# A blocked Strassen matmul with bias and tanh: three hand-set orders moved around the change from plain to Strassen work

## The chip, the cores and the metric

One core of a Trainium2 chip. The metric is the device time of one launch in microseconds (us), the median of three runs. An engine's "queue" is the order in which its instructions stand in the program: each engine takes them one after the other, and a waiting instruction holds up all behind it.

## The reference

```python
m, k, n = 4096, 4096, 4096
a: float32 [m, k];  b: float32 [k, n];  bias: float32 [n]
return np.tanh(np.matmul(a, b) + bias)
```

## The kernel before

The output is made in four column blocks of 1024 and sixteen row pairs of 256 rows. One such piece of 256 x 1024 is an **item** (`items`, indexed by `n`). An item is computed by Strassen's scheme in its Winograd-like form: seven products `m1` to `m7` of half size (128 x 2048 by 2048 x 512), each 16 matmuls on TensorE (PE), line 339. The left operands are the quarters `a11`, `a12`, `a21`, `a22` of the item's rows and their differences `s1`, `s2`, `s5`, `s6`, `s7` (`asum`, line 89, on VectorE, DVE); the right operands are `b11`, `b22` and the sums `d1`, `d3`, `d4`, `e6`, `e7`. `a11` and `a12` come from the first 128 rows of the item (`r = 0`), `a21` and `a22` from the second (`r = 1`).

Rows of `a` come from HBM by DMAs on GpSimd's queue (POOL), cast to float16 (`load_nat`, line 147): two tiles (`u` = 0, 1) of four DMAs each for every `r`. VectorE turns them (`turn`, `transpose`, line 174) into the layout that TensorE needs; each quarter takes a turn from `u` = 0 and one from `u` = 1. The tiles lie in the pool `wide` with eight buffers, which also holds the raw blocks `b12` and `b21`.

The first three row pairs of the first column block are computed plainly before any item, in the groups A, B and C of two row blocks each (`ROWS`), four row blocks at a time in the eight PSUM banks, while `b` still arrives. The visits follow `ORDER`; the last, to group A, is `last_visit`, in two parts (columns `j` = 0, 1) between the first item's products. When a row block is finished, `end(m, j)` applies tanh on ScalarE (ACT, line 671) into an output tile and stores it from SyncE's queue (SP, line 350). Output tiles come from `new_out()` (pool `outs`, three buffers) or from `narrow()`, which goes round the spare buffers of `temps` and `outs`.

What comes when is written by hand. Time is counted in **slots**: `at_slot(slot, f, ...)` lists work for a slot, and the main loop goes through the slots, emits the slot's listed work, then a visit if the slot is negative, and then the slot's products. Items stand 7 slots apart. Where several calls have the same slot, they come in the order in which they were listed. `prepare(n)` lists an item's loads, turns and sums:

```python
loads = {0: (-5, -4), 1: (0, 2), 2: (3, 5)}.get(n, (s0 - 7, s0 - 4))
for r in range(2):
    at_slot(loads[1 - r], load_nat, n, r)
```

The first two items (`n < LEAD`) have an order of products of their own: m4 (slot 7n), m2 (+2), m3 (+4), m1 (+5), m5 (+6), m6 (+8), m7 (+10). From the third item on it is m2 (7n), m5 (+2), m3 (+4), m1 (+5), m4 (+6), m6 (+8), m7 (+10). Products of neighbouring items interleave. After a product its banks are read out: `lead_after` and `lead_add` for the first two items, `after` for the others. For the third item, `after("m2")` puts two reads of m2's bank on VectorE (to `d` and to `s`), and m5 goes on accumulating in that bank only behind both. `lead_bias(n)` copies the bias into the bank of m4 on ScalarE; `lead_add(n)` adds m2's copy `zs` to it, applies tanh (`result`, line 359), stores it, and copies the bank to `ds`.

Of the kernel before, what the change touches and what calls it, by code (L numbers as in the profile page):

```python
# [8 lines left out]
P = 128  # L9
QP = 32  # L10
NB = 512
# [6 lines left out]
fp32 = mybir.dt.float32  # L18
# [5 lines left out]
TANH = mybir.ActivationFunctionType.Tanh  # L24
# [30 lines left out]
ROWS = {"A": (0, 1), "B": (2, 3), "C": (4, 5)}  # L55
# [5 lines left out]
def kernel(  # L61
# [7 lines left out]
    nc = tc.nc  # L69
# [11 lines left out]
    wide = ctx.enter_context(tc.tile_pool(name="wide", bufs=8))  # L81
# [39 lines left out]
    def again(n):  # L121
        return items[n][3]
# [38 lines left out]
    def quad(n, name):  # L161
        if name not in aset[n]:
            aset[n][name] = quads.tile([P, T, P], fp16, name=name, tag=name)
        return aset[n][name]

    def transpose(dst, src, lowest):

        nb = src.shape[2]
        split = [(0, nb, "P mb b (t x) -> P mb b t x")]
        if lowest:  # L170
            split = [(0, 1, "P mb b (x t) -> P mb b t x"), (1, nb - 1, split[0][2])]
        for b0, n, order in split:
            if n:
                nc.vector.transpose(  # L174
                    dst[:, ds(b0 * TB, n * TB), :].rearrange(
                        "P (b t) (mb p) -> P mb b t p", t=TB, p=QP
                    ),
                    src[:, :, ds(b0, n), :].rearrange(order, t=TB),
                )

    def turn(n, name, u):
        c, pairs, part, _ = items[n]
        r, h = int(name[1]) - 1, int(name[2]) - 1
        src = nat[n, r, u].rearrange("P mb (b h k) -> P mb b h k", h=2, k=TB * QP)[:, :, :, h, :]
        if part is None:
            dst = quad(n, name)[:, :, ds(u * 2 * QP, 2 * QP)]
        else:
            dst = quad(n, name)[:, ds(u * TP, TP), :]
        transpose(dst, src, h == 0 and not part)

    def stored(n, name):
        c, pairs, part, _ = items[n]
# [156 lines left out]
    def store(o, pair, r, c, j):  # L349
        nc.sync.dma_start(  # L350
            out=out[ds((2 * pair + r) * P, P), ds(c * NCW + j * NB, NB)], in_=o
        )

    def new_out():
        return outs.tile([P, NB], fp32, name="o", tag="o")
# [112 lines left out]
    def at_slot(slot, f, *args):  # L468
        work.setdefault(slot, []).append((f, args))

    def prepare(n):

        s0 = SLOTS * (n - 1)
        if again(n):
            at_slot(s0, lambda: aset[n].update((i, aset[n - 2][i]) for i in QUADS))
        elif natural(n):
            loads = {0: (-5, -4), 1: (0, 2), 2: (3, 5)}.get(n, (s0 - 7, s0 - 4))
            for r in range(2):
                at_slot(loads[1 - r], load_nat, n, r)
            turns = {  # L480
                0: (("a22", (-2, -1)), ("a21", (-2, -1)), ("a11", (2, 3)), ("a12", (2, 4))),
                1: (("a22", (5, 6)), ("a21", (5, 6)), ("a11", (8, 9)), ("a12", (8, 9))),
                2: (("a22", (10, 10)), ("a21", (11, 11)), ("a11", (12, 12)), ("a12", (13, 13))),
            }.get(n, [(i, (s0 + x, s0 + y)) for i, (x, y) in {
                "a22": (0, 0), "a21": (2, 2), "a11": (3, 4), "a12": (5, 5)
            }.items()])
            for name, at in turns:
                for u in range(2):
                    at_slot(at[u], turn, n, name, u)
                if n:  # L490
                    at_slot(at[1], keep, n, name)
        else:
            for name, at in (("a22", 0), ("a21", 1), ("a11", 2), ("a12", 4)):
                at_slot(s0 + at, fetch, n, name)
        late = stays(n)
        end_ = n == len(items) - 1
        sums_at = {"s2": 4, "s5": 6, "s1": 9}
        sums_at["s6"] = 12 if late else 13 if end_ else 8
        sums_at["s7"] = 15 if late else 12 if end_ else 13
        if n < LEAD:  # L500
            at_slot(s0 + 10, lead_add, n)
        if n == 0:
            sums_at = {"s2": 6, "s1": 10, "s5": 11, "s6": 14, "s7": 16}
        elif n == 1:
            sums_at = {"s2": 6, "s1": 9, "s5": 9, "s6": 13, "s7": 14}
        elif n == 2:
            sums_at.update({"s2": 5, "s5": 6})
        for name, at in sums_at.items():
            at_slot(s0 + at, asum, n, name)
# [20 lines left out]
    mb = {}  # L530
# [31 lines left out]
    def narrow(name):  # L562
        pool, tag = rest[taken[0] % len(rest)]
        taken[0] += 1
        return pool.tile([P, NB], fp32, name=name, tag=tag)
# [50 lines left out]
    for m in range(4):  # L616
        src = a[ds(m * P, P), :].rearrange("p (q k) -> p q k", q=4)[:, :, ds(0, TB * QP)]
# [4 lines left out]
        if m == 1:  # L622
            nc.gpsimd.affine_select(
                out=ident, in_=ident, compare_op=mybir.AluOpType.is_equal, fill=0.0,
# [4 lines left out]
    for t in range(0, TB, 2):  # L629
        for q in (0, 2, 1, 3):  # L630
            src = bass.AP(
                tensor=b.tensor, offset=b.offset + (q * KQ + t) * N,
                ap=[[TB * N, QP], [N, 2], [1, NCW]],
            )
# [31 lines left out]
            mb[m, j] = psum.tile([P, NB], fp32, name=f"ps_{2 * m + j}", tag=f"ps_{2 * m + j}")  # L666
    banks = [mb[i] for i in ((3, 0), (0, 0), (2, 1), (1, 0), (2, 0), (0, 1), (3, 1), (1, 1))]

    def end(m, j):
        o = new_out() if m in ROWS["A"] else narrow("o")  # L670
        nc.scalar.activation(o, mb[m % 4, j], TANH)
        store(o, m // 2, m % 2, 0, j)

    def visit(v):
        g = ORDER[v]
# [26 lines left out]
    def last_visit(j):  # L702
        for m in ROWS["A"]:
            down(m, j, 7 * TB, 8 * TB, stop=True)
            end(m, j)

    for slot, f, *args in (
        (-22, turn_in, "C0", (4, 5)),
        (-21, add_bias, 2, False), (-21, add_bias, 3, False),
        (-20, add_bias, 0, True), (-20, add_bias, 1, True),  # L710
        (-20, land, "C2", 4, TP, TP), (-20, opening_b, 3),
        (-19, turn_in, "B1", (2, 3), TB, TB), (-19, turn_in, "B1", (2, 3), TP, TB),
        (-18, turn_in, "A1", (0, 1), TB, TB), (-18, turn_in, "A1", (0, 1), TP, TB),
        (-17, land, "B3", 2, 3 * TB, TP), (-17, land, "A3", 0, 3 * TB, TP), (-17, opening_b, 4),
        (-17, add_bias, 4, True), (-17, add_bias, 5, True), (-17, bsum, "d4", 0),
        (-16, turn_in, "C2", (4, 5)),
        (-15, land, "C4", 4, T, TP), (-15, opening_b, 5),
        (-15, bsum, "d3", 0), (-15, bsum, "e6", 0), (-14, bsum, "d1", 0), (-14, bsum, "e7", 0),
        (-13, turn_in, "B3", (2, 3), 3 * TB, TB), (-13, turn_in, "B3", (2, 3), T, TB),
        (-13, turn_in, "A3", (0, 1), 3 * TB, TB), (-13, turn_in, "A3", (0, 1), T, TB),  # L720
        (-12, land, "B5", 2, 5 * TB, TP), (-12, land, "A5", 0, 5 * TB, TP), (-12, opening_b, 6),
        (-12, bsum, "d4", 1), (-12, bsum, "d3", 1), (-11, bsum, "e6", 1), (-11, bsum, "d1", 1),
        (-10, turn_in, "C4", (4, 5)), (-10, bsum, "e7", 1),
        (-9, land, "C6", 4, 6 * TB, TP), (-9, opening_b, 7),
        (-9, bsum, "d4", 2), (-8, bsum, "d3", 2), (-8, bsum, "e6", 2),
        (-7, turn_in, "B5", (2, 3)), (-7, turn_in, "A5", (0, 1)),
        (-6, land, "B7", 2, 7 * TB, TB),
        (-6, bsum, "d1", 2), (-6, bsum, "e7", 2),
        (-4, turn_in, "C6", (4, 5)), (-4, land, "A7", 0, 7 * TB, TB),
        (-3, bsum, "d4", 3), (-3, bsum, "d3", 3), (-3, bsum, "d1", 3),  # L730
        (-2, turn_in, "B7", (2, 3)),
        (0, turn_in, "A7", (0, 1)), (0, bsum, "e6", 3), (1, bsum, "e7", 3),
        (5, lead_bias, 1),
    ):
        at_slot(slot, f, *args)

# [3 lines left out]
    for c in range(1, NC):  # L740
        n = next(n for n in range(len(items)) if items[n][0] == c)
# [4 lines left out]
    for slot in range(1 - len(ORDER), SLOTS * len(items) + 4):  # L746
        for f, args in work.get(slot, ()):
            f(*args)
        if slot < 0:
            visit(slot + len(ORDER) - 1)  # L750
        elif slot in (1, 3):
            last_visit(slot // 2)
        for pos, p in PRODUCTS.items():
            n, r = divmod(slot - pos, SLOTS)
            if r == 0 and 0 <= n < len(items):
                if n < LEAD:
                    product(n, *PRODUCTS[FIRST[pos]])
                elif n < len(items) - 1 or p[0] not in ("m6", "m7"):
                    product(n, *p)
                elif p[0] == "m6":  # L760
                    product(n, *PRODUCTS[10])
                else:
                    last_product(n, *PRODUCTS[8][1:])
# [30 lines left out]
```

## Time and profile before

| | us |
|---|---|
| median of three runs (1578.27 to 1578.87) | 1578.69 |
| the profiled execution's own time | 1580.22 |
| its span | 1578.5 |
| TensorE busy in the span | 1569.0 |
| VectorE busy | 925.5 |
| GpSimd busy (issue of DMAs) | 354.8 |
| ScalarE busy | 286.6 |
| mean granted TensorE clock | 0.999 |

A row of a timeline gives start, length, engine, line, operation, written and read tile, and count; in brackets stands the idle time of the engine before it and what ended it. The name `ps` is any PSUM bank, `s` a difference of `a`, `a` a turned quarter, `nat` rows as they land.

### The profile page before, as it was taken

What the parts mean: (1) busy time and instruction counts of PE and PEld (TensorE: products, weight loads), DVE (VectorE), ACT (ScalarE), POOL (GpSimd) and SP (SyncE); (2) the same over time, 40 slices, a digit from 0 to 9 for tenths busy, and PEclk for the clock granted to TensorE, in tenths of its full rate; (3) what the DMA queues carried; (4) which work ended last, traced back from release to release, by engine and by line L of the source; (5) the groups of instructions that cost most, each with busy time, mean ns of one, the idle gap of its engine ahead of it and who ended that gap; (6) DMA issues with size and microseconds to landing.
All of it is one profiled execution on the core that took longest, in us unless ns stands there. A gap on an engine that the chain in (4) does not pass through costs nothing.

```text
span 1578.5 us, 18906 instructions
## 1 busy us (share of the span) xinstructions
PE 1569.0 (99%) x7276; PEld 711.0 (45%) x7276; DVE 925.5 (59%) x1070; ACT 286.6 (18%) x506; POOL 354.8 (22%) x664
## 2 busy tenths in 40 slices
PE   9999999999999999999999999999999999999999
PEld 4444444444444444444444444444444444444444
DVE  6789777777975566577794333333468433333332
ACT  3431111111221111111222111111122111111111
POOL 8766343334441222133430000000140000000000
PEclk9999999999999999999999999999999999999999
DMA  9999887889896776589985444444494444444441
GB/s 177 178 233 247 196 169 167 184 180 234 169 212 182 192 186 173 161 211 227 192 168 162 137 124 140 133 125 142 124 198 116 137 133 134 127 140 133 120 140 55
DMA packets 152989, 258.83 MB, mean 164 GB/s; under 512 B 21826, under 2 KB 72770, under 8 KB 152900
## 3 DMA queue, kind: packets, MB, share of 16 engines
q0 software_dynamic: 83248, 85.89, 36.0%
q1 hardware_dynamic: 69504, 171.60, 32.9%
q8 instruction: 57, 0.93, 0.2%
q14 instruction: 32, 0.26, 0.1%
q10 hardware_dynamic: 148, 0.14, 0.0%
HBM read 242.75 MB, written 100.66 MB: 218 GB/s over the span
## 4 chain that ended last, share of the span: by engine, by line
PE 90%; DMA 5%; POOL 2%; DVE 1%; issue 1%; DVEq 0%; ACT 0%; POOLq 0%; ACTq 0%
PE ps L339 90%; DMA nat<-in_a_dram 2%; DMA land<-in_a_dram 1%; DMA b<-in_b_dram 1%; POOL land L588 1%; POOL nat L147 1%; POOL b L243 1%; DVE a L174 1%; DMA side<-in_b_dram 0%; DVE ao L174 0%; PE ps L315 0%; DVE s L89 0%; DVE ps L89 0%; POOL first L621 0%; POOL side L635 0%
## 5 line engine op out<-in xcount | busy, mean ns | idle before, releaser
L339 PEld LDWEIGHTS <-a 128*128 128x128 f16 x3696 | 361.3, 98 | 438.3 <-DVE a L174 2.8
L339 PEld LDWEIGHTS <-s 128*128 128x128 f16 x3120 | 305.7, 98 | 371.7 <-issue 4.6
L339 PE MATMUL ps<-d,a 128*128 128x512 f16 x1952 | 441.2, 379 | 1.5 <-DVE a L174 1.5
L339 PE MATMUL ps<-b,s 128*128 128x512 f16 x1708 | 391.2, 380 | 2.1 <-DVE s L89 2.1
L339 PE MATMUL ps<-e,a 128*128 128x512 f16 x1528 | 348.1, 379 | 0.0
L89 DVE TENSOR_TENSOR s<-a,a 128x2048 f16<-128x2048 f16 x195 | 236.3, 1213 | 13.2 <-DMA a<-scratch 12.0
L174 DVE STREAM_TRANSPOSE a<-nat 128x1024 f16<-128x1024 f16 (+3 forms) x256 | 214.9, 883 | 13.1 <-PE ps L339 9.3
L147 POOL DMA_DIRECT2D nat<-in_a_dram x288 | 152.0, 533 | 310.8 <-DVE a L174 241.7
L339 PE MATMUL ps<-d,s 128*128 128x512 f16 x976 | 220.6, 379 | 0.0
L359 ACT ACTIVATE o<-ps 128x512 f32<-128x512 f32 x180 | 108.1, 601 | 312.4 <-issue 290.8
L243 POOL DMA_DIRECT2D b<-in_b_dram x236 | 127.5, 547 | 131.2 <-PE ps L339 40.1
L89 DVE TENSOR_TENSOR ps<-cs,ps 128x512 f32<-128x512 f32 (+1 forms) x62 | 42.2, 686 | 185.4 <-PE ps L339 185.4
L89 DVE TENSOR_TENSOR a<-a,a 128x2048 f16<-128x2048 f16 x110 | 133.7, 1216 | 0.0
L89 DVE TENSOR_TENSOR ps<-ps,bias_bc 128x512 f32<-128x512 f32 x63 | 43.5, 695 | 131.9 <-PE ps L339 131.9
L89 DVE TENSOR_TENSOR ps<-ps,s 128x512 f32<-128x512 f32 x71 | 48.6, 695 | 122.3 <-PE ps L339 111.9
L89 DVE TENSOR_TENSOR o<-ds,ps 128x512 f32<-128x512 f32 x61 | 41.8, 685 | 121.3 <-PE ps L339 89.4
L420 ACT ACTIVATE o<-o 128x512 f32<-128x512 f32 x59 | 37.2, 630 | 365.3 <-DVE o L89 365.3
L405 ACT COPY ds<-ps 128x512 f32<-128x512 f32 x59 | 34.6, 586 | 302.0 <-PE ps L339 302.0
L243 POOL DMA_DIRECT2D side<-in_b_dram x12 | 6.4, 543 | 316.7 <-PE ps L339 316.5
L339 PE MATMUL ps<-side,s 128*128 128x512 f16 x268 | 68.8, 379 | 0.0
L339 PE MATMUL ps<-side,a 128*128 128x512 f16 x216 | 55.4, 379 | 0.0
L379 ACT COPY cs<-ps 128x512 f32<-128x512 f32 x59 | 34.6, 586 | 106.8 <-PE ps L339 106.8
(71 smaller groups left out, 549.5 us busy)
## 6 DMA issues: line engine op xcount, KB each, us to landing
out_dram<-o SPq DMA_DIRECT2D x255, 256.0 KB, 4.2
a<-scratch SPq DMA_DIRECT2D x124, 512.0 KB, 4.6
nat<-in_a_dram POOLq DMA_DIRECT2D x352, 128.0 KB, 6.6
b<-in_b_dram POOLq DMA_DIRECT2D x236, 128.0 KB, 6.1
scratch<-a SPq DMA_DIRECT2D x48, 512.0 KB, 7.0
scratch<-a SPq DMA_DIRECT2D x32, 256.0 KB, 6.3
land<-in_a_dram POOLq DMA_DIRECT2D x40, 128.0 KB, 5.1
a<-scratch SPq DMA_DIRECT2D x16, 256.0 KB, 3.5
```

The lines of the kernel that those rows point to most:

```text
L89: nc.vector.tensor_tensor(out=out_, in0=in0, in1=in1, op=op)
L147: nc.gpsimd.dma_start(out=tl[ds(q * QP, QP), :, :], in_=src.rearrange("(mb p) k -> p mb k", p=QP),)
L174: nc.vector.transpose(dst[:, ds(b0 * TB, n * TB), :].rearrange("P (b t) (mb p) -> P mb b t p", t=TB, p=QP), src[:, :, ds(b0, n), :].rearra ...
L243: nc.gpsimd.dma_start(out=dst[ds(q * QP, QP)], in_=src)
L339: nc.tensor.matmul(st[where], at, bt, start=(what == "m2" or n < LEAD and what == "m1") and i == 0, stop=i == len(ts_) - 1, skip_group_che ...
L359: nc.scalar.activation(o, src, TANH)
L379: nc.scalar.copy(st["cs"], st["c"])
L405: nc.scalar.copy(st["ds"], st["d"])
L420: nc.scalar.activation(o, o, TANH)
L588: nc.gpsimd.dma_start(out=tl[ds(q * QP, QP)], in_=src.rearrange("(mb p) k -> p mb k", p=QP))
```

## The change

- The last turn of the first item's `a22` (from `u` = 1) is done in two pieces, the first quarter of its columns and the rest.
- Both loads of the second item go to slot 4 (before: 0 and 2), both of the third to slot 5 (before: 3 and 5).
- The fourth item's `a22` is turned in slot 15 (before: 14), and the second item's `s7` is made in slot 15 (before: 14). The third item's m2 and the VectorE reads of its bank are emitted at the end of slot 14.
- The ends of group C go into two tiles of the pool `wide` instead of tiles of `narrow()`, and are stored by four DMAs on GpSimd's queue, emitted in slot -1, behind the first item's loads. The output tiles of group A come from `new_out()` except the last, of B from `narrow()`.
- Both parts of group A's last visit come in slot 3 (before: one in slot 1 and one in slot 3), so that the first item's m2 follows its m4.

```diff
-    def transpose(dst, src, lowest):
+    def transpose(dst, src, lowest, soon=False):
         nb = src.shape[2]
         split = [(0, nb, "P mb b (t x) -> P mb b t x")]
-        if lowest:
-            split = [(0, 1, "P mb b (x t) -> P mb b t x"), (1, nb - 1, split[0][2])]
+        if lowest or soon:
+            one = "P mb b (x t) -> P mb b t x" if lowest else split[0][2]
+            split = [(0, 1, one), (1, nb - 1, split[0][2])]
...
-        transpose(dst, src, h == 0 and not part)
+        transpose(dst, src, h == 0 and not part, (n, name, u) == (0, "a22", 1))
...
-            loads = {0: (-5, -4), 1: (0, 2), 2: (3, 5)}.get(n, (s0 - 7, s0 - 4))
+            loads = {0: (-5, -4), 1: (4, 4), 2: (5, 5)}.get(n, (s0 - 7, s0 - 4))
...
+                3: (("a22", (15, 15)), ("a21", (16, 16)), ("a11", (17, 18)), ("a12", (19, 19))),
...
-            sums_at = {"s2": 6, "s1": 9, "s5": 9, "s6": 13, "s7": 14}
+            sums_at = {"s2": 6, "s1": 9, "s5": 9, "s6": 13, "s7": 15}
...
+    ends = {}
     def end(m, j):
-        o = new_out() if m in ROWS["A"] else narrow("o")
+        if m in ROWS["C"]:
+            if m not in ends:
+                ends[m] = wide.tile([P, 2, NB], fp32, name="ends", tag="wide")
+            nc.scalar.activation(ends[m][:, j], mb[m % 4, j], TANH)
+            return
+        o = narrow("o") if m in ROWS["B"] or (m, j) == (1, 1) else new_out()
         nc.scalar.activation(o, mb[m % 4, j], TANH)
         store(o, m // 2, m % 2, 0, j)
+    def store_ends():
+        for j in range(2):
+            for m in ROWS["C"]:
+                nc.gpsimd.dma_start(
+                    out=out[ds(m * P, P), ds(j * NB, NB)], in_=ends[m][:, j]
+                )
...
-        (5, lead_bias, 1),
+        (-1, store_ends), (5, lead_bias, 1),
...
-        elif slot in (1, 3):
-            last_visit(slot // 2)
+        elif slot == 3:
+            last_visit(0)
+            last_visit(1)
```

## The prediction

> Products are written with their item, m4(0) being the first item's m4; "rows r=1" are the second 128 rows of an item's row pair.
>
> **What bounds the kernel now.** I read the page's busy line, then the waits of PE, then PE's timeline around each wait.
>
> ```profile
> PE 1569.0 (99%) x7276; PEld 711.0 (45%) x7276; DVE 925.5 (59%) x1070; ACT 286.6 (18%) x506; POOL 354.8 (22%) x664
> ...
> PE ps L339 <- DVE s L89: 2.1, 1, 2.1
> PE ps L339 <- DVE a L174: 1.5, 2, 0.8
> ```
>
> PE is the bound: 99% busy. What any reordering can win is PE's idle time, and the waits of the whole run that touch L339 are three: 3.6 us. PE's timeline places them.
>
> ```profile
> 91.84 3.63 PE L339 MATMUL ps<-d,a 128*128 128x512 f16 x16 [0.80 <-DVE a L174]
> ...
> 103.12 3.63 PE L339 MATMUL ps<-d,a 128*128 128x512 f16 x16 [0.73 <-DVE a L174]
> 106.58 3.62 PE L339 MATMUL ps<-d,s 128*128 128x512 f16 x16
> ...
> 113.49 3.62 PE L339 MATMUL ps<-d,a 128*128 128x512 f16 x16
> ...
> 146.86 5.30 PE L339 MATMUL ps<-b,s 128*128 128x512 f16 x16 [2.08 <-DVE s L89]
> 152.00 3.62 PE L339 MATMUL ps<-e,a 128*128 128x512 f16 x16
> 155.45 3.62 PE L339 MATMUL ps<-d,a 128*128 128x512 f16 x16
> ```
>
> In order: m4(0) waits 0.80 for the turned a22; m3(0) waits 0.73 for a11; m1(0); m4(1) without a wait; m5(2) waits 2.08 for the second read-out of m2(2); m7(1); m3(2). Products follow each other every 3.45 us (155.45 - 152.00), but m5(2) takes 5.14: its 16 matmuls fall in a stretch of half clock.
>
> ```profile
> 115.00:125.00 10.00, 10.00 (x48) 4.44 (x47) 10.00 (x13) 1.23 (x2) 7.76 (x15) 1.00 1.11 219
> ...
> 145.00:155.00 10.00, 8.14 (x30) 3.32 (x30) 8.38 (x12) 0.47 (x1) 6.43 (x13) 0.83 1.11 235
> ```
>
> The columns are PE, PEld, DVE, ACT, POOL (busy and count), granted clock, DMA share. The clock is 0.83 where m5(2) stalls: the stall costs 2.08 + (5.14 - 3.45) = 3.8. DVE is full (10.00 of 10) and so are the DMA engines (share over 1), while POOL issues 15 loads in 10 us, 0.67 each. So this stage has three full resources, and the order of each counts. After 155 PE has no wait at all.
>
> [...]
>
> **What the change wins, step by step.**
>
> - m4(0): four 256 KB stores leave SP's queue just as the rows for a22 arrive, and the last turn of a22 is cut in two (0.41 + 0.93, instead of 1.2 before the first matmul). The copy of the bias into its bank on ACT (L427, 90.74 + 0.59) stays ahead of m4(0): start 91.4, gain 0.4.
> - m2(0) moves to 94.9 (91.4 + 3.45). Its s2 ends at 94.2 before (93.00 + 1.23), so it is covered by 0.6. Both last visits (1.73 each) follow, then m3(0) at 101.8. Its rows r=0 landed at 102.4 (DVE's turn starts at 102.62); with four transfers of about 0.65 fewer beside them, about 99.5. The 0.73 goes.
> - m5(2): its read-outs start at 145.56 behind s7(1) (1.22) and the two turns of a22(3) (2.37); both go behind them, 3.6 earlier. The 3.8 goes if nothing else holds DVE. s7(1) is then done 1.2 after the read-outs, 3.5 before m7(1) needs it.
> - The four activations into the wide buffers cost ACT the same 0.6 each, and the buffers (of b12 and b21, block 2) are long free.
>
> Were that all, 0.4 + 0.7 + 3.8 = 4.9 us would be won.
>
> **What it makes late.** Two edits look free and aren't.
>
> *First, the output buffers.* ACT's order is now: zs, the result of lead_add(0), its copy, then the four ends of group A. The third of these, end(0,1), rotates onto the buffer that lead_add's result has just filled, so ACT waits until that store has landed; m1(0) waits for end(0,1), since it overwrites that bank. Queued behind it on ACT are end(1,1), m3(0)'s copy to cs and lead_bias(1).
>
> ```profile
> 104.55 0.60 ACT L359 ACTIVATE o<-ps 128x512 f32<-128x512 f32 x1 [2.46 <-DVE ps L89]
> ...
> DMA to landing us min/median/max: 6.2/7.2/8.1
> ```
>
> The first line is lead_add's result now, the second the landing of SP's stores issued from 97 to 108. The result comes some 3 us earlier with its rows, so it ends at 102; + 6.2 = 108.2; + 0.6 for end(0,1): m1(0) can start at 108.9. PE is there at 101.8 + 3.45 = 105.2, and idles 3.6. m1(0) and m5(0) then end at 115.8, or 117.5 with one stretch of half clock.
>
> *Second, the rows of the second item.* load_nat is called for r=0 and then r=1; with both at slot 4, the r=0 rows are issued first. Before they came last. But a22(1) and a21(1) are r=1, and are turned first.
>
> ```profile
> 88.31 0.54 POOL L147 DMA_DIRECT2D nat<-in_a_dram  x1 [0.31 <-issue]
> ...
> 102.71 0.53 POOL L147 DMA_DIRECT2D nat<-in_a_dram  x1 [0.53 <-DMA nat<-in_a_dram]
> ...
> 113.84 0.53 POOL L147 DMA_DIRECT2D nat<-in_a_dram  x1 [0.85 <-DMA nat<-in_a_dram]
> ```
>
> Count POOL's DMAs from 88.31, the first of the first item's r=0 rows. Number 16, at 102.71, closed the second item's r=1 rows and landed 6.5 later, at 109.2. In the new order come 8 loads, 4 stores, 8 loads of r=0, 8 of r=1: number 28 closes them. Number 28 was issued at 113.84 and landed 5.1 later, at 118.9. Four of the 28 are now stores that formerly shared the engines from SP's queue, so four transfers fewer are ahead: 4 x 0.65 = 2.6 us earlier, 116.3. That a store takes as long as a load on this queue no row shows; a load's 0.65 is the nearest, 1.3 the upper bound (twice that, the store having twice the bytes in SBUF). DVE reaches the last turn just then (the half before lands some 2.7 earlier, and its turns and the read-out of m1(0) take 2.42 + 0.69), so a22(1) is turned at t = 116.4 + 1.24 = 117.7. Before:
>
> ```profile
> 110.92 2.42 DVE L174 STREAM_TRANSPOSE a<-nat 128x1024 f16<-128x1024 f16 x3
> ...
> 148.99 2.48 DVE L174 STREAM_TRANSPOSE a<-nat 128x256 f16<-128x256 f16 x4
> 152.20 0.70 DVE L89 TENSOR_TENSOR ps<-ps,s 128x512 f32<-128x512 f32 x1 [0.73 <-PE ps L339]
> ```
>
> There it was turned at 112.15 (110.92 + 1.23). From then to the end of the a21(3) turns at 151.47 DVE worked 39.3 us with 0.65 idle. All of that work is still ahead of the read-out of m5(2), only permuted, and m3(2) needs this read-out. So m3(2) starts at t + 39.3 + 0.7 + 0.1 = t + 40.1. PE's own way is shorter: m4(1) at t, m6(0) at t + 4.8 (s6(0) ended 116.93, 4.8 after 112.15), nine products to m7(1) at t + 35.9, m3(2) at t + 39.4. So up to 0.7 of half clock, plus the 1.4 before m6(0), is hidden. m3(2) started at 155.45 before, and behind it PE has no wait in either order as DVE idles again from there.
>
> **Sum.** t + 40.1 - 155.45 = t - 115.35; with t = 117.7, +2.3 us. All gains are inside this number: they shorten a way that now waits. The profiled execution took 1580.22 (span 1578.5 and 1.7 around it), 1.5 more than the median of 1578.69; the difference is put on the median: **1581.0**.
>
> **Rivals.**
>
> 1. *Only the buffer wait holds* (0.15). If the r=1 rows land by 113.9 (where t - 115.35 is 0) or sooner, PE goes on at 115.8 and m7(1) starts at 115.8 + 34.5 = 150.3 against 152.00: -1.7, or 0 with half clock. For it: 20 DMAs at 0.65 behind a landing at 99.5 end at 112.5 if SP's stores took nothing. Against it: five of SP's stores fall in that time. 1577.0 to 1578.7.
> 2. *The full gain* (0.08), faster: the r=1 rows are turned by 112.0 and the store lands within 3 us, and m1(0) and m4(1) don't wait. Point of decision: landing at 110.7. Then -4.9: 1573.8. Against: from 99.5 to 110.7 there is room for 17 landings at 0.65 with nothing from SP, and 20 are needed.
> 3. *Stores cost more on POOL's queue* (0.22), slower: at 1.3 each they put number 28 at 118.9 and t at 120.3: +4.9, 1583.6. It takes the case out of the 0.2% above 0.65 + 0.9 / 4 = 0.87 per store. POOL's pace of 0.83 from 100 to 105 (6 issues in 5 us), with SP's stores beside it, speaks for it. A second stretch of half clock at m4(1) behind m1(0)'s adds up to 1.
>
> That the edit undoes itself, the loads' order being the reverse of the need, is the forecast itself (0.55).
>
> **Numbers.** Within 0.2% (3.2 us, about what a measurement tells from no change) lie rival 1 and most of the forecast: 0.64. Slower: rival 3 and the forecast's upper edge, 0.28. Faster: rival 2, 0.08. The range reaches from rival 1's end (1577.0) to rival 3's (1583.8) and leaves out rival 2 and some of the upper tail.
>
> **What would show it.** In PE's waits of the changed kernel: m5(2) without its 2.1; a wait of some 3.6 at about 109 on ACT's o (m1(0)); one of 0 to 2 at about 118 on DVE's a (m4(1)), and small ones at m6(0) and m3(2). In the clock, half speed near 109, none near 147. DVE idle from about 105 to 113. If m4(1) starts before 115, the count on POOL's queue is wrong; if m1(0) starts before 106, the buffer step is.

## The result, and the profile after

The changed kernel takes 1583.76 us (median of 6 runs, 1582.89 to 1586.44), the kernel before 1578.48 in the same comparison (6 runs, 1577.33 to 1580.03): a ratio of 1.0036, 95% interval 1.0023 to 1.0049. It is 5.3 us slower. The forecast was 2.3 slower; 1583.76 lies at the upper edge of its range.

The busy line of the page after:

```profile
PE 1569.8 (99%) x7276; PEld 711.7 (45%) x7276; DVE 925.2 (59%) x1071; ACT 286.4 (18%) x506; POOL 356.8 (23%) x668
```

PE works 0.8 us longer in a span of 1581.0, against 1569.0 in 1578.5. The rest of the 2.5 is waiting. The waits of PE (what waits, for what; total us, times, longest):

```profile
PE ps L340 <- ACT o L681: 3.5, 1, 3.5
PE warm L611 <- DVE zeros L275: 1.3, 1, 1.3
PE ps L340 <- DVE a L89: 1.2, 1, 1.2
PE ps L340 <- DVE a L175: 1.1, 1, 1.1
PE ps L340 <- ACT ps L428: 0.3, 1, 0.3
PE ps L340 <- DVE ps L89: 0.3, 1, 0.3
```

m5(2)'s wait for `s` (2.1) has gone and so have the 1.5 for turned quarters at m4(0) and m3(0). In their place stand 3.5 at m1(0) for an output tile of ACT (`end`, L681), 1.1 at m4(1) and 1.2 at m6(0). PE's timeline, at m4(0), m3(0), m1(0), m5(0), m4(1), m6(0), m7(1) and m3(2):

```profile
91.31 3.61 PE L340 MATMUL ps<-d,a 128*128 128x512 f16 x16 [0.34 <-ACT ps L428]
...
101.67 3.62 PE L340 MATMUL ps<-d,a 128*128 128x512 f16 x16
108.77 5.07 PE L340 MATMUL ps<-d,s 128*128 128x512 f16 x16 [3.48 <-ACT o L681]
113.68 3.62 PE L340 MATMUL ps<-b,s 128*128 128x512 f16 x16
118.42 3.63 PE L340 MATMUL ps<-d,a 128*128 128x512 f16 x16 [1.13 <-DVE a L175]
123.20 1.04 PE L340 MATMUL ps<-side,a 128*128 128x512 f16 x4 [1.15 <-DVE a L89]
...
154.29 3.62 PE L340 MATMUL ps<-e,a 128*128 128x512 f16 x16
158.22 3.61 PE L340 MATMUL ps<-d,a 128*128 128x512 f16 x16 [0.31 <-DVE ps L89]
```

m3(2) starts at 158.22 instead of 155.45, 2.8 later. The rest of the span behind that start is 1422.8 here and 1423.05 before, and between 1422.7 and 1423.1 in every profile of this study that shows the stage. So one number stands for a kernel's span: the start of m3(2). The time adds what lies around the span, and that differs too, by the medians of the runs: 1.7 us in the kernel before and 1.9 after, but 2.1 in the ninth experiment and 2.3 to 2.4 in the first, third, eighth, tenth and twelfth. Why is not shown.

By windows (columns PE, PEld, DVE, ACT, POOL, granted clock, DMA share, GB/s):

```profile
105.00:115.00 10.00, 6.52 (x25) 2.53 (x24) 2.25 (x4) 2.06 (x4) 5.66 (x11) 0.83 1.06 244
115.00:125.00 10.00, 7.72 (x36) 3.19 (x35) 9.25 (x12) 0.63 (x1) 7.27 (x15) 1.00 1.12 211
145.00:155.00 10.00, 10.00 (x48) 4.57 (x47) 9.96 (x11) 1.23 (x2) 4.25 (x8) 1.00 1.10 261
```

The half clock has moved from 145-155 (0.83 before) to 105-115, where DVE now works 2.25 of 10 us. Both late steps can be seen on the queues. ACT first, with lead_add's result, the first two ends of group A, and the third behind its wait:

```profile
102.14 0.60 ACT L360 ACTIVATE o<-ps 128x512 f32<-128x512 f32 x1 [1.84 <-DVE ps L89]
102.63 0.58 ACT L437 COPY ds<-ps 128x512 f32<-128x512 f32 x1
103.09 1.11 ACT L681 ACTIVATE o<-ps 128x512 f32<-128x512 f32 x2
108.12 1.09 ACT L681 ACTIVATE o<-ps 128x512 f32<-128x512 f32 x2 [3.92 <-DMA out_dram<-o]
```

`end(0,1)` waits 3.92 for the landing of lead_add's store, and m1(0) starts 0.65 behind its start. Then DVE, at the turns of a22(1):

```profile
104.40 1.22 DVE L89 TENSOR_TENSOR s<-a,a 128x2048 f16<-128x2048 f16 x1
113.38 2.43 DVE L175 STREAM_TRANSPOSE a<-nat 128x1024 f16<-128x1024 f16 x3 [7.75 <-DMA nat<-in_a_dram]
115.73 0.67 DVE L89 TENSOR_TENSOR ps<-cs,ps 128x512 f32<-128x512 f32 x1
117.12 2.43 DVE L175 STREAM_TRANSPOSE a<-nat 128x1024 f16<-128x1024 f16 x3 [0.72 <-DMA nat<-in_a_dram]
```

It idles 7.75 until the first half of the r=1 rows is there, and 0.72 again for the second, which landed at 117.0. Between the two stands the read-out of m1(0) (115.73), which needs that product and the copy `cs` of m3(0). So both late ways meet on DVE: the last turn of a22(1) waits for the rows, and for the read-out ahead of it. As in the prediction, t is the end of this turn (118.37).

### The profile page after: what moved, and what is told of

It is laid out like the page before. It is cut to its first block, busy times and chain, and to the rows that moved or that the text cites. A ratio compares the mean times of both kernels' runs of the same rounds, so it can differ in the third digit from the quotient of the medians.

```text
span 1581.0 us, 18901 instructions
## 1 busy us (share of the span) xinstructions
PE 1569.8 (99%) x7276; PEld 711.7 (45%) x7276; DVE 925.2 (59%) x1071; ACT 286.4 (18%) x506; POOL 356.8 (23%) x668
## 4 chain that ended last, share of the span: by engine, by line
PE 91%; DMA 5%; POOL 2%; DVE 1%; issue 1%; ACT 0%; DVEq 0%; ACTq 0%
PE ps L340 90%; DMA nat<-in_a_dram 3%; DMA b<-in_b_dram 1%; POOL nat L147 1%; POOL land L590 1%; DMA land<-in_a_dram 1%; DVE a L175 1%; POOL b L244 1%; PE warm L611 0%; PE ps L549 0%; PE ps L316 0%; DVE ao L175 0%; DVE ps L89 0%; PE spread L301 0%; DVE d L89 0%
```

## The experiments

The theory, from the prediction: two ways are late at the same place, ACT's wait for a buffer ahead of m1(0), and the second item's r=1 rows behind its r=0 rows. Rivals: one of them alone; stores dear on POOL's queue; the half clock. "Rows closed" is the time by which the last of the second item's r=1 rows has landed. Every ratio is against the kernel before in the same comparison. Its medians there were 1579.42 (33 runs, first to fourth experiment), 1580.1 (35, fifth to eighth) and 1579.56 (33, ninth to twelfth).

**1. The r=1 rows first again.**

```diff
-            for r in range(2):
+            for r in (1, 0):
```

> The changed kernel, except that load_nat is called for r=1 ahead of r=0 (all the rest of the change stays). Theory 'rows': the second item's r=1 rows come too late on POOL's queue and set the time. Then number 20 of POOL's DMAs closes them instead of number 28, eight landings of 0.65 to 0.8 earlier, at about 111; m4(1) starts when PE gets there, at 115.8 to 117.5, with no wait on DVE, and only the wait of 3.5 at m1(0) is left: 3 us under the changed kernel, about 1580.5. Rival 'buffer': the wait of m1(0) on the output buffer sets the time; then no change, 1583.8. Rival 'stores': the four stores on POOL's queue are what is dear; then no change or under 1 us.

Measured: 1582.38, ratio 1.0016 (1.0006 to 1.0025); m3(2) at 157.94; 1580.5 was expected. The rows closed at 110.5 and m4(1) needs no wait, but it starts at 119.44, because m1(0) waits longer than in the kernel after. The waits of PE in this kernel, then its window, then DVE's read-out of m1(0):

```profile
PE ps L340 <- ACT o L681: 4.9, 1, 4.9
```

```profile
105.00:115.00 10.00, 5.09 (x14) 1.74 (x13) 4.04 (x5) 2.27 (x5) 6.31 (x12) 0.66 1.05 231
```

```profile
116.25 0.70 DVE L89 TENSOR_TENSOR ps<-cs,ps 128x512 f32<-128x512 f32 x1 [6.54 <-PE ps L340]
```

lead_add's store landed at 109.5 here (108.0 after). The half clock lasted 6.83 us, two stretches on end (a granted clock of 0.66 over 10 us). The read-out waits 6.54 for m1(0), and behind it the last turn ends at t = 118.10, hardly before the 118.37 of the kernel after. So the buffer wait alone costs most of the loss. How much depends on the half clock: six of the twelve runs have a granted clock of 0.999 (median 1580.68), six of 0.998 (1583.12), and the profile is one of the latter.

**2. The buffers alone.** The narrow buffer goes to tile (0,1), which m1(0) waits for, and (1,1) takes the one behind lead_add's.

```diff
-        o = narrow("o") if m in ROWS["B"] or (m, j) == (1, 1) else new_out()
+        o = narrow("o") if m in ROWS["B"] or (m, j) == (0, 1) else new_out()
```

> The changed kernel, except that end(0,1) takes the narrow tile and end(1,1) one of the three output tiles, so that end(0,1) no longer waits for the landing of lead_add's store. Theory 'rows': m1(0) starts at 105.1 without a wait, PE comes to m4(1) at 112 and waits there about 6 us instead of 1.1: the same time as the changed kernel within 1 us (1583 to 1584.5). Rival 'buffer': 3.5 us under it, 1580.3.

Measured: 1584.65, ratio 1.0028 (1.0019 to 1.0038); m3(2) at 160.22. m1(0) goes on at 105.68, and the same loss appears at m4(1); PE's waits and its timeline there:

```profile
PE ps L340 <- DVE a L175: 7.1, 1, 7.1
...
PE ps L340 <- ACT o L681: 0.4, 1, 0.4
```

```profile
119.84 6.01 PE L340 MATMUL ps<-d,a 128*128 128x512 f16 x16 [7.09 <-DVE a L175]
```

The rows closed at 118.4, t is 119.78. So the row order alone costs the whole loss as well.

**3. Both edits of 1 and 2.**

> The changed kernel with both edits: r=1 rows first, and end(0,1) in the narrow tile. Theory 'rows and buffer together': no wait at m1(0), m4(1), m6(0) or m5(2) is left; only the 0.35 at m4(0): 4 to 5 us under the kernel before, 1573.5 to 1574.5, the full gain of rival 2 in the prediction. Rival 'stores': the stores on POOL's queue still hold up the second item's rows, which land at about 111 against 110.7 needed: a wait of up to 2 us at m4(1), 1575 to 1577.

Measured: 1577.28, ratio 0.9987 (0.9977 to 0.9997), by a narrow margin faster than before, but not the 1573.5 to 1574.5 that was expected. Rows closed at 112.2, m1(0) at 107.18 after a wait of 0.41, m4(1) at 114.72 after 0.47, no half clock between 84 and 160. The two waits lie on ways that meet in front of the last turn of a22(1); taking away either shows the other, and only both together give the time back.

**4. PE kept busy in the gap**, by 16 matmuls of zeros that are added to m3(0)'s bank behind m3(0).

```diff
+            if (n, what) == (0, "m3"):
+                for _ in range(16):
+                    nc.tensor.matmul(
+                        st[where], zeros[:, :P], zeros, start=False, stop=True,
+                        skip_group_check=True,
+                    )
```

> The changed kernel with 16 more matmuls of zeros by zeros, added to m3(0)'s bank right behind m3(0), so that PE is busy during most of the wait at m1(0); the output stays the same. Theory 'rows': a22(1) is turned no sooner, so m4(1) starts at the same 118.4; no half clock near 109; the time is that of the changed kernel within 0.5 us. Rival 'clock': the half clock behind the wait at m1(0) is what makes the timed runs 2.6 us dearer than the two profiles' difference; then 1 to 1.7 us under the changed kernel.

Measured: 1583.79, ratio 1.0024 (1.0014 to 1.0034), no different from the kernel after. PE's timeline at m1(0) and m4(1):

```profile
110.94 3.61 PE L340 MATMUL ps<-d,s 128*128 128x512 f16 x16 [1.74 <-ACT o L687]
...
120.44 5.31 PE L340 MATMUL ps<-d,a 128*128 128x512 f16 x16 [2.43 <-DVE a L175]
```

The half clock near 109 has gone (granted clock 1.00 from 105 to 115), and m1(0) takes 3.6 us. But the rows closed at 119.0, m4(1) waited for them and the half clock came there (0.83 from 115 to 125). In seven of the ten runs the granted clock is 1.000, and their median is 1583.61: without any half clock in this stage the loss is the same. So the half clock is not the limit.

**5 and 6. The kernel before and the kernel after once more**, in one comparison with the next two.

> The kernel before, unchanged, profiled and timed once more. Theory 'landing': the rows of this stage land up to 2 us earlier or later from execution to execution; a22(1) has its rows by 109 to 110 and no wait of over 0.5 at m4(1). Theory 'phase': the stretch of half clock that cost 1.7 of the stall at m5(2) falls on it only in a part of the executions; without it a profile shows m5(2) with 16 matmuls in 3.6 and a span of about 1576.5 to 1577.

Measured: 1579.86, ratio 0.9996 (0.9985 to 1.0008). m5(2) waits 2.08 again, with the half clock behind it (granted clock 0.83 from 145 to 155); PE's timeline:

```profile
145.85 5.30 PE L339 MATMUL ps<-b,s 128*128 128x512 f16 x16 [2.08 <-DVE s L89]
```

But m4(0) waits 0.34 for the bias, not 0.80 for a22, and m3(0) not at all, while m1(0) waits 0.63 for ACT's `o`: the first item's r=0 rows landed at 99.4 (102.4 in the first profile). m3(2) starts at 154.44, a full microsecond earlier than in the profile that the prediction was made from.

> The changed kernel, unchanged, profiled and timed once more. Theory 'landing': number 28 of POOL's DMAs lands at 118 to 119 where the first profile had 117.0; m4(1) starts at 119.5 to 120.5 and the span is 1582 to 1583.5. Theory 'phase': it lands at 117 again, and the span is over 1582 because of a second stretch of half clock between 108 and 122.

Measured: 1583.73, ratio 1.0018 (1.0007 to 1.0029). In this execution the buffer wait is the longer of the two (PE's m3(0), m1(0), m4(1); then DVE's read-out of m1(0), its last turn of a22(1) and the read-out ahead of m3(2)):

```profile
101.91 3.63 PE L340 MATMUL ps<-d,a 128*128 128x512 f16 x16 [0.25 <-DVE a L175]
110.94 5.93 PE L340 MATMUL ps<-d,s 128*128 128x512 f16 x16 [5.40 <-ACT o L681]
...
120.16 3.62 PE L340 MATMUL ps<-d,a 128*128 128x512 f16 x16
```

```profile
116.98 0.69 DVE L89 TENSOR_TENSOR ps<-cs,ps 128x512 f32<-128x512 f32 x1 [0.26 <-PE ps L340]
117.88 2.43 DVE L175 STREAM_TRANSPOSE a<-nat 128x1024 f16<-128x1024 f16 x3 [0.21 <-DMA nat<-in_a_dram]
...
158.26 0.67 DVE L89 TENSOR_TENSOR ps<-ps,s 128x512 f32<-128x512 f32 x1
```

lead_add's store went out at 104.0 and landed at 110.2; the half clock lasted 6.83 (granted clock 0.69 from 105 to 115, 0.97 from 115 to 125). The rows closed at 117.8, and m4(1), at 120.16, no longer waits for them. But the last turn does, by 0.21: t is 119.13, and m3(2) starts at 158.98, 39.85 behind it as in the first profile of after (158.22 - 118.37). So DVE's way, and with it the rows, still sets the time here; PE's late m4(1) is hidden.

**7. The later loads alone**, in the kernel before.

```diff
-            loads = {0: (-5, -4), 1: (0, 2), 2: (3, 5)}.get(n, (s0 - 7, s0 - 4))
+            loads = {0: (-5, -4), 1: (4, 4), 2: (5, 5)}.get(n, (s0 - 7, s0 - 4))
```

> The kernel before, with the new slots of the loads alone: both of the second item at 4, both of the third at 5, so r=0 rows come first. Theory 'rows': number 24 of POOL's DMAs closes the second item's r=1 rows at 116 to 117 (116.4 in the kernel before); m4(1) waits 3 to 5 us on DVE's a; the wait at m5(2) stays, as its order is the old one: 4 to 6 us over the kernel before, 1583 to 1585. Rival 'stores': loads alone cost under 1 us.

Measured: 1584.58, ratio 1.0026 (1.0016 to 1.0037), as slow as the whole change. PE's waits:

```profile
PE ps L339 <- DVE a L174: 4.1, 1, 4.1
PE ps L339 <- DVE s L89: 1.7, 1, 1.7
```

The rows closed at 115.5 (109.2 and 108.0 in the two profiles of before), without one of the stores on POOL's queue: the loads do it, and by their order, since with the r=1 rows first they closed at 110.5 in the first experiment. m1(0) waits only 0.45 here: in the old order of buffers and visits its tile waits for an older store (0.93 on ACT), not for lead_add's.

**8. Rows ahead of the stores.** The third experiment's kernel, with the r=1 loads at slot 0 and the four stores behind them.

```diff
-            loads = {0: (-5, -4), 1: (4, 4), 2: (5, 5)}.get(n, (s0 - 7, s0 - 4))
+            loads = {0: (-5, -4), 1: (0, 4), 2: (5, 5)}.get(n, (s0 - 7, s0 - 4))
...
-        (-1, store_ends), (5, lead_bias, 1),
+        (1, store_ends), (5, lead_bias, 1),
```

> The changed kernel with the narrow tile for end(0,1), r=1 rows first and at slot 0, and the four stores of group C behind them (slot 1) on POOL's queue. Theory 'landing': the r=1 rows land four transfers earlier than with the stores ahead of them (112.2 there), at about 109.5; the waits of 0.5 at m4(1) and 1.2 at m6(0) go: 1 to 2 us under that kernel (1577.3), 1575.3 to 1576.3, and no half clock in the stage. Rival 'engines full': the order on the queue changes nothing because all transfers share the engines; 1577.3.

Measured: 1578.08, ratio 0.9987 (0.9976 to 0.9998). The rows closed at 106.7, yet m4(1) still waits 1.30 and m6(0) 1.15; m3(2) at 153.06. What holds them is not the rows: ACT's timeline, then DVE's.

```profile
110.27 0.60 ACT L681 ACTIVATE o<-ps 128x512 f32<-128x512 f32 x1 [5.41 <-DMA out_dram<-o]
110.77 0.58 ACT L448 COPY cs<-ps 128x512 f32<-128x512 f32 x1
```

```profile
111.38 0.70 DVE L89 TENSOR_TENSOR ps<-cs,ps 128x512 f32<-128x512 f32 x1 [3.24 <-ACT cs L448]
111.98 2.42 DVE L175 STREAM_TRANSPOSE a<-nat 128x1024 f16<-128x1024 f16 x3
```

The tile (1,1) now waits for lead_add's store. Queued behind it on ACT is the copy of m3(0) to `cs`; DVE's read-out of m1(0) needs that, and the last turn of a22(1) stands behind the read-out. The 0.47 of the third experiment has the same cause: its rows had closed at 112.2, and the read-out waited 2.09 for `cs`, until 112.82.

**9. The read-outs ahead of the turns alone**, in the kernel before.

```diff
+                3: (("a22", (15, 15)), ("a21", (16, 16)), ("a11", (17, 18)), ("a12", (19, 19))),
...
-            sums_at = {"s2": 6, "s1": 9, "s5": 9, "s6": 13, "s7": 14}
+            sums_at = {"s2": 6, "s1": 9, "s5": 9, "s6": 13, "s7": 15}
```

> One part alone on the kernel before: only the read-outs of the third item are put ahead of the turns of the fourth (the turns of the fourth item and s7 of the second one step or more later). My theory says that this part does what it was meant to do and is independent of the rest: m5(2)'s wait of 2.08 us and the 1.7 us that the half clock behind it takes go, m3(2) starts at about 151.7 to 153.4 instead of 154.4 to 155.5, and the time falls by 2.1 to 3.8 us against the kernel before in the same comparison. The rival, that what is saved there is waited for again right behind (by m3(2) or m7(2)), gives the time of before, with m3(2) at 154.4 to 155.5.

Measured: 1576.77, ratio 0.9985 (0.9973 to 0.9996). From m1(0) to m3(2) there is no wait but m3(2)'s own, in PE's timeline:

```profile
106.26 3.61 PE L339 MATMUL ps<-d,s 128*128 128x512 f16 x16 [0.66 <-ACT o L672]
...
151.67 3.61 PE L339 MATMUL ps<-d,a 128*128 128x512 f16 x16 [0.30 <-DVE ps L89]
```

m3(2) starts 3.78 ahead of the first profile of before. Of this 0.33 came by earlier rows (t is 111.82 here, 112.15 there); the part's own gain is the 3.45 from t on. The ten runs with a granted clock of 1.000 have a median of 1576.72, the 18 such runs of before 1578.70: without the half clock the part is worth 2.0. This one part is what the change was good for.

**10. The tile (1,1) behind `cs`**, in the eighth experiment's kernel.

```diff
-            end(m, j)
+            if (m, j) != (1, 1):
+                end(m, j)
...
-        (1, store_ends), (5, lead_bias, 1),
+        (1, store_ends), (5, lead_bias, 1), (5, end, 1, 1),
```

> The seventh experiment's kernel with one instruction of ACT moved: the tanh of the last tile of the last visits (1,1), which waits for the landing of lead_add's store at 110.2, comes behind the copy of m3(0)'s sum (cs) and lead_bias(1) instead of ahead of them. If the 1.30 us of m4(1) and the 1.15 us of m6(0) there come from that queue (cs late, so DVE's read-out of m1(0) late, so the last turn of a22(1) behind it late), cs is ready at about 105.5, the turn at about 110.5, m4(1) starts at 111.9 without a wait, m6(0) waits 0 to 0.6, m3(2) starts at 150.6 to 151.2, and the time is 1.9 to 2.5 us below that of the seventh experiment (whose median was 1578.1 beside 1580.1 of before, so 1575.6 to 1576.2 on that scale; 3.6 to 4.5 below before). The rival, that m4(1) waits for its rows in any case, leaves the wait of 1.3 and the time of the seventh experiment.

Measured: 1576.65, ratio 0.9983 (0.9974 to 0.9992), the lowest of the study. ACT's timeline, then all that is left in PE's waits of the products:

```profile
105.81 0.59 ACT L448 COPY cs<-ps 128x512 f32<-128x512 f32 x1 [0.18 <-ACT o L681]
106.29 0.59 ACT L428 COPY ps<-bias_bc 128x512 f32<-128x512 f32 x1
111.20 0.60 ACT L681 ACTIVATE o<-ps 128x512 f32<-128x512 f32 x1 [4.32 <-DMA out_dram<-o]
```

```profile
PE ps L340 <- ACT ps L428: 0.3, 1, 0.3
PE ps L340 <- DVE ps L89: 0.3, 1, 0.3
```

The wait for the landing is still there, 4.32 us long, and costs nothing, since nothing that PE needs is queued behind it. m4(1) starts at 112.58, m6(0) at 116.07, m3(2) at 151.08. So the 1.30 and the 1.15 were ACT's queue. That this kernel beats the ninth experiment's, in which the stores, buffers and visits are as before, is not shown: their intervals overlap.

**11. The third group's stores back on SP's queue**, in the third experiment's kernel (narrow buffers, stored as they are done).

```diff
-        if m in ROWS["C"]:
...
-        o = narrow("o") if m in ROWS["B"] or (m, j) == (0, 1) else new_out()
+        o = narrow("o") if m not in ROWS["A"] or (m, j) == (0, 1) else new_out()
...
-        (-1, store_ends), (5, lead_bias, 1),
+        (5, lead_bias, 1),
```

> The third experiment's kernel (changed kernel, rows in the old order, the buffers of two tiles exchanged) with the third group's stores put back on SP's queue, one by one as the tiles are done, from narrow buffers. My theory holds the place of these stores for a small matter: the stores start 5 to 10 us earlier and share the engines with the first item's rows, so m4(0) or m3(0) wait up to 0.7 us more, and the time is 0 to 1.5 us above that of the third experiment. The rival of the prediction, that stores are dear on POOL's queue, says that the time falls by up to 4.9 us against the third experiment and the second item's rows close well before 112.2.

Measured: 1578.51, ratio 0.9992 (0.9983 to 1.0001); the third experiment had 0.9987. Its profiled execution took 5615.63 us, a span of 5613.9 with 1.3 of waits of PE in it, and shows nothing of this stage, so only the ten other runs speak (1576.2 to 1580.6). Putting these stores back on SP's queue won nothing, and no 4.9 us; by median spans it lost (1576.7, 1574.9 in the third experiment). It is a weak test of their price, since in the third experiment the rows were no longer last.

**12. The last visits in their old places**, in the third experiment's kernel.

```diff
-        elif slot == 3:
-            last_visit(0)
-            last_visit(1)
+        elif slot in (1, 3):
+            last_visit(slot // 2)
```

> The third experiment's kernel with the two last visits in their old places (one behind m2(0), one behind m4(0)), so m2 is not next to m4. The four buffers of the last tiles are then taken in an order in which none waits for lead_add's store. My theory: no wait of ACT for a landing near 104 to 110; m4(0) and m3(0) wait as in before (0.8 and 0.7) or less; m4(1)'s 0.47 and m6(0)'s 1.15 go or stay; time from 1.5 us below to 0.5 us above the third experiment. If setting m2 next to m4 was itself worth something (the two gains of 0.4 and 0.7 that the prediction counted), the time is 0.7 to 1.1 above the third experiment.

Measured: 1578.28, ratio 0.9992 (0.9983 to 1.0001). No end waits for a landing any more, m4(0) waits 0.34 and m3(0) not at all; m4(1) waits 1.34, because the rows closed at 112.0, and m6(0) 1.15. The times can't be told from the third experiment's.

All in one table (the end t of the last turn of a22(1), m4(1)'s start, its wait, the longest run of half clock near m1(0) to m4(1), m3(2)'s start, and how far it lies behind t):

| kernel | rows closed | t | m4(1) | its wait | half clock | m3(2) | m3(2) - t |
|---|---|---|---|---|---|---|---|
| before, first profile | 109.2 | 112.15 | 113.49 | 0 | 0 | 155.45 | 43.30 |
| before, again | 108.0 | 111.14 | 112.48 | 0 | 0 | 154.44 | 43.30 |
| read-outs ahead alone (9) | 109.5 | 111.82 | 113.16 | 0 | 0 | 151.67 | 39.85 |
| after, first profile | 117.0 | 118.37 | 118.42 | 1.13 | 3.41 | 158.22 | 39.85 |
| after, again | 117.8 | 119.13 | 120.16 | 0 | 6.83 | 158.98 | 39.85 |
| rows repaired alone (1) | 110.5 | 118.10 | 119.44 | 0 | 6.83 | 157.94 | 39.84 |
| buffers repaired alone (2) | 118.4 | 119.78 | 119.84 | 7.09 | 6.83 | 160.22 | 40.44 |
| PE filled (4) | 119.0 | 120.38 | 120.44 | 2.43 | 3.41 | 160.22 | 39.84 |
| both repaired (3) | 112.2 | 114.66 | 114.72 | 0.47 | 0 | 154.50 | 39.84 |
| both, rows ahead of stores, (1,1) behind `cs` (10) | 107.3 | 111.23 | 112.58 | 0 | 0 | 151.08 | 39.85 |

With the read-outs ahead, m3(2) starts 39.84 or 39.85 behind t, whatever PE waits for; DVE works between them without a new gap. The one exception is the second experiment: its two stretches of half clock (granted clock 0.66 from 115 to 125) fall on m4(1) itself, and PE comes 0.6 later than DVE.

## Why the prediction was right in its mechanism and short in its size

*The gains.* m5(2)'s stall is gone in every kernel with the read-outs ahead. It was put at 3.8; from t to m3(2) the gain is 3.45 (43.30 - 39.85), as m3(2) now waits 0.3 itself, and it is smaller still in an execution without the half clock. That the two profiles in the ninth experiment differ by 3.78 is partly luck. The 0.4 at m4(0) and the 0.7 at m3(0) were there in the profiles (waits of 0.34 and 0), but were not the change's doing: the kernel before has them too when its rows land earlier, as its second profile shows.

*First, the output buffers.* Right in kind and place: 3.48 at 108.77 on ACT's `o`, where 3.6 at 108.9 was forecast. In the repeat it was 5.40 at 110.94, as lead_add's store landed at 110.2 instead of the forecast's 108.2, and the half clock made m1(0) 5.8 long (116.71 - 110.94, 2.3 more than the usual 3.45) where 1.7 more was the most that the sum allowed. That this way is hidden behind the other was right even so: m3(2) kept its 39.85 behind t. But only just, as the read-out of m1(0) ended 0.2 ahead of the last rows there.

*Second, the rows.* Right in kind, and m3(2) = t + 40.1 was right within 0.25 (39.85). Too early was t itself.

*The steps that failed.* Measured were +5.3 in the first comparison (6 runs each; 3.6 to 7.7 by the interval of the ratio) and +3.6 in the second (1583.73 - 1580.1; 12 and 35 runs; 1.1 to 4.6). The forecast was 1581.0, +2.3. Two of its steps were too small, and one a little too large.

The first is "four transfers fewer are ahead: 4 x 0.65 = 2.6 us earlier, 116.3", and with it t = 117.7. Number 28 landed at 117.0 and 117.8 in the two profiles of after, and at 118.4 and 119.0 in the second and fourth experiments, whose loads and stores stand on POOL's queue in the same order. So 1.9 to none of the 2.6 was there. In the changed kernel t was 118.37 and 119.13, 0.7 and 1.4 too late for the forecast. The first profile, 1582.89, is one of the fastest of 18 runs (1582.58 to 1586.44); the repeat, 1583.73, is the median of its twelve. Why these rows land so differently is open.

The second is "the difference is put on the median". The sum gives m3(2) at 157.8 (117.7 + 40.1), and with the rest of the span (1423.05) and the 1.7 around it 1582.5; the forecast took off 1.5, because before's median lay that far below its profiled execution. But that execution had paid for the half clock at m5(2), and many others had not. In the three later comparisons the granted clock is 1.000 in 47 of 101 runs of before (medians 1577.99, 1578.09 and 1578.70), and 0.999 or less in the other 54 (1580.5, 1581.0 and 1581.6); the profiles with no half clock in this stage list 1.000, those with one or two stretches 0.999 or 0.998. So the stall at m5(2), 2.08 in both profiles of before, costs 1.7 more in about half of the executions only, while the changed kernel pays for its late rows always. (The granted clock of a run doesn't tell where its half clock fell; that it was at m5(2) is read from the two profiles.) The half clock explains 1.7 of the 2.5 to 2.9 between the two kinds of run; the waits of 0.80 and 0.73 for the first item's rows, which the second profile of before has shorter (0.34 and 0, with 0.63 at m1(0) instead, and m3(2) 1.0 earlier), may be part of the rest.

With both put right, and 39.85 for 40.1, the sum is 1581.0 + 1.4 + 1.5 - 0.25 = 1583.7 with the t of the repeat.

*Rivals.* Rival 1 was priced wrongly: with the rows in time, the buffer wait alone (first experiment) gives +3.0 against before, not -1.7 to 0. It followed PE's way alone and left out DVE's, where the read-out of m1(0), and behind it the last turn, wait for m1(0) to end; and it took no account of two stretches of half clock. Rival 2's full gain is what the tenth experiment reaches between profiles (span 1578.5 to 1573.9, -4.6 of the 4.9), but 2.9 between medians, since half of the runs of before have no half clock to lose and 0.6 more lies around the span. Rival 3 had nearly the measured number, 1583.6, but not the cause. It priced a store on POOL's queue at 1.3: in the seven profiles with the four stores ahead of the second item's loads, these landed 0.58 to 1.10 apart behind the first item's last row (0.76 over all seven), and the loads alone, without a store on that queue, cost as much as the whole change (seventh experiment).

## What to carry to other kernels

When a trace shows two late arrivals in front of the same instruction, price each with the other taken away, since repairing one shows only the other (+3.0 and +5.2 alone, -2.1 together). Before a load is moved in a queue, look up which part of it is used first; and before a wait is put into an engine's queue, what stands behind it there, for a wait with nothing urgent behind it is free, as the 4.32 us in the tenth experiment were. A single profile is one draw: compare its time with the median and its granted clock with that of the other runs, and price a new limit against the waits that a usual execution has.

## What the runs showed of the hardware

In the first profile of before the granted clock was 1.00 from 4.14 to 147.50, 0.50 from 147.50 to 150.91 and 1.00 from there to 1577; in that of after it was 1.00 from 5.94 to 108.34, 0.50 from 108.34 to 111.75 and 1.00 from there to 1580. The two stretches of half clock are 3.41 long, and the full clock ahead of them, 143.36 and 102.40 us, is a whole number of such lengths (143.36 / 42 = 102.40 / 30 = 3.413). In the other profiles the granted clock of 10 us gives the length: 0.83 is one stretch of 3.41 (0.17 x 10 / 0.5 = 3.4), 0.66 is two (6.8).

The stalls, and what came with them (in us):

| kernel and stall | length | granted clock | stretches of half clock |
|---|---|---|---|
| seventh, m5(2) | 1.71 | 1.00 (145 to 155) | none |
| fourth, m1(0) | 1.74 | 1.00 (105 to 115) | none |
| before (both profiles), m5(2) | 2.08 | 0.83 (145 to 155) | one |
| fourth, m4(1) | 2.43 | 0.83 (115 to 125) | one |
| after, m1(0) | 3.48 | 0.83 (105 to 115) | one |
| seventh, m4(1) | 4.13 | 0.83 (115 to 125) | one |
| first, m1(0) | 4.91 | 0.66 (105 to 115) | two |
| after again, m1(0) | 5.40 | 0.69, 0.97 (105 to 115, 115 to 125) | two |
| second, m4(1) | 7.09 | 0.66 (115 to 125) | two |

So the stalls of 1.71 and 1.74 us brought no half clock, those of 2.08 to 4.13 one stretch, and those of 4.91 to 7.09 two. The two profiles of before and after also show where the idle time lay: in the 3.41 us that end where the half clock starts, PE was idle for 2.08 in before (144.09 to 147.50) and for 3.05 in after (104.93 to 108.34). The last 0.43 of after's stall lay in the half clock itself, and the clock behind it was 1.00.

As an estimate from these two profiles: if steps of 3.41 lie fixed in time, and a stall counts by what falls into one of them, a stall of 2.08 lies inside a single step in 1.3 of 3.41 cases (3.41 - 2.08), and brings no half clock in the others, unless a part of it is enough. That is 0.39 of the cases or more; 54 of 101 runs of before, 0.53, have a granted clock below 1.000. No run tests the estimate itself.

The landings of one program lay 1 to 3 us apart between two executions, with a DMA share of 1.06 to 1.12 in the windows of after above: the first item's r=0 rows landed at 99.4 and 102.4 in the two profiles of before, and lead_add's store 5.2 and 6.2 us behind its issue in the two of after.
